# Dot products of fetched expert rows placed behind the gates' first pass

## The chip, the cores and the metric

The kernel runs on one core of a Trainium2 chip. The metric is the device time of one execution in microseconds; lower is better. Five engines run their own instruction queues and wait for each other through semaphores: TensorE (PE in the profile, its weight loads PEld), VectorE (DVE), ScalarE (ACT), GpSimd (POOL) and SyncE (SP), which only issues transfers here. Each engine works through its queue in the order in which the compiler's scheduler has put it.

## What is computed

One layer of a decoder step over 512 prompt tokens and 32 sample tokens: a mixer (retention and a convolution module, one input and one output projection), a layer norm, then a retrieval of experts, a second norm. The change lies in the retrieval:

```python
q = (xb @ w_query).reshape(PEER_BLOCK, PEER_HEADS, PEER_DQ)
...
s1 = jnp.einsum('phd,hkd->phk', q1, sub_keys_1)
s2 = jnp.einsum('phd,hkd->phk', q2, sub_keys_2)
v1, i1 = lax.top_k(s1, PEER_TOPK)
v2, i2 = lax.top_k(s2, PEER_TOPK)
...
idx = e1 * N_KEYS + e2
gate = jax.nn.softmax(sv.astype(jnp.float32), axis=-1).astype(xb.dtype)
u = jnp.take(peer_u, idx, axis=0)
act = jax.nn.gelu(jnp.einsum('phkd,pd->phk', u, xb), approximate=False)
vv = jnp.take(peer_v, idx, axis=0)
return jnp.einsum('phk,phkd->pd', gate * act, vv)
```

There are 8 heads with 16 picks each, so every token takes 128 of 16,384 experts. Each expert has a row of 1,024 numbers in `peer_u` and one in `peer_v`.

## The kernel before

The tokens are treated in two ways.

**Fetched rows.** The first chunk of 128 prompt tokens, the 32 samples (group "s") and the second chunk of 128 prompt tokens (group "b") fetch the rows of the experts they picked. `gather` does this, one slot at a time. A slot is: an indirect transfer by POOL's queue (L564) of one row pair of 8 KB for each of 128 partitions into a tile `g`, of which the pool has three buffers; on DVE the dot product of the `u` half with the token (L567); on ACT the Gelu and its product with the gate (L569, L570); on DVE the weighted add of the `v` half into `acc` (L575). The first chunk has 128 slots, started in the mixer and done before the part that follows here. The samples are folded onto 128 partitions and have 32 slots, the second chunk has 128. `fetched()` runs these two groups one after the other, each closed by sums over the folded parts (samples only, L933 and L934), a residual add (L582), the norm of L445 to L453 and a store by SP (L585).

**Dense scores.** The last two chunks, 256 tokens, are computed against all experts instead, 128 blocks of 128 experts. `scores_of` loads a block of `u` (L771) and multiplies (L774); Gelu follows on ACT; `place(e)` is the block's slice of one of four tiles, Gb, Gc, Ga and Gd (32, 20, 44 and 32 blocks). Then the scores are multiplied by the gates, which are zero but for the picked experts, and `v_stage` multiplies the result with a block of `v` rows loaded by SP (L889) and adds it up in four PSUM tiles `pB` (L893). The loads of both kinds share five buffers.

**The gates.** `build` makes the gate matrix for eight tokens at a time. DVE compares indices and writes one-hot tiles A (L847), M (L849) and B (L852), two buffers each; PE multiplies them, three matmuls a token (L858), into one of two PSUM tiles; DVE drains each PSUM tile. `first_keys` is the first pass, over the 96 blocks of Gb, Gc and Ga, with 96 columns a matmul: three instructions drain four tokens (L870 once, L872 twice). `last_keys` is the second pass, over the 32 blocks of Gd, drained by ACT (L878). The blocks of Gc and Gd have their scores computed after their gates: `s_stage` puts Gelu into W (ACT, L884) and multiplies it in on DVE (L885).

**Order.** The source calls the first pass, then `run` interleaves `phases()` (one block of `v_stage`, at times with an `s_stage` or a step of the second pass) with two steps of `fetched()`. This is not yet the order on the engines: a scheduler places each instruction by its dependencies and by modelled times, so that slots of the samples come ahead of the first pass and in the middle of it on DVE. `behind(ins, other)` is a helper that forbids the scheduler to put `ins` ahead of `other`; it adds no data. At the end two layer norms read `pB` and store the last two chunks.

Of the kernel before, what the change touches and what calls it, by code (L numbers as in the profile page):

```python
# [14 lines left out]
OP = mybir.AluOpType  # L15
# [3 lines left out]
D = 1024  # L19
# [72 lines left out]
def tile_step(ctx: ExitStack, tc: tile.TileContext, a, o):  # L92
    nc = tc.nc
    V, S, T, G = nc.vector, nc.scalar, nc.tensor, nc.gpsimd
# [68 lines left out]
    def behind(ins, other):  # L163
        tc.add_manual_dep(ins.ins, other.ins.name, mybir.DependencyInfo(
            mybir.DependencyClass.NoSync, mybir.DependencyReason.DATA), reason="order")
# [297 lines left out]
    def mix_mm(n, gT, y, c0, wo, xT=None):  # L463

        banks_ = [mmps(), mmps()]
        if xT is not None:
            for q in range(2):
                residual(banks_[q], xT, range(q * 4, q * 4 + 4), c0)
        for src, k0 in ((y, 4), (gT, 0)):
            for q in range(2):  # L470
                for s in range(2):
                    for k in range(4):
                        last = T.matmul(banks_[q][:n, s * 256:(s + 1) * 256], src[:, k, c0:c0 + n],
                                        wo[q * 2 + s][:, k0 + k, :], start=(xT is None and k0 == 4 and s == 0 and k == 0),
                                        stop=(k0 == 0 and s == 1 and k == 3), skip_group_check=True)
        return banks_, last
# [31 lines left out]
    def retrieve(q_of, hs, w, r, E, gate, e0, later=None):  # L508
# [47 lines left out]
        V.reciprocal(sm[:n], sm[:n])  # L556
        V.tensor_mul(gate[:n, e0:e0 + nh], ex[:n], sm[:n].unsqueeze(2).to_broadcast([n, nh, TK]))

    def gather(x1, idx, gate, acc, slots):

        for k in slots:
            t = (gx.tile([128, 2 * D], F32, name="g") if x1 is x1_0 and k < KX and k % 4 == 3 else
                 gp.tile([128, 2 * D], F32, name="g"))
            G.indirect_dma_start(out=t, out_offset=None, in_=a["uv"],  # L564
                                 in_offset=bass.IndirectOffsetOnAxis(ap=idx[:, k:k + 1], axis=0))
            act = gw.tile([128, 2], F32, name="act")
            V.scalar_tensor_tensor(t[:, :D], t[:, :D], 1.0, x1, op0=OP.mult, op1=OP.mult, accum_out=act[:, 0:1])  # L567
            wgt = gw.tile([128, 1], F32, name="wgt")
            S.activation(act[:, 1:2], act[:, 0:1], AF.Gelu)  # L569
            S.activation(wgt, act[:, 1:2], AF.Copy, scale=gate[:, k:k + 1])  # L570
            v = t[:, D:]
            if k == slots[0]:
                S.activation(acc, v, AF.Copy, scale=wgt)
            else:
                V.scalar_tensor_tensor(acc, v, wgt, acc, op0=OP.mult, op1=OP.add)  # L575
            yield
# [10 lines left out]
    def run(*gens):  # L587

        live = list(gens)
        while live:  # L590
            for g in list(live):
                for _ in range(g[1]):
                    if next(g[0], "end") == "end":
                        live.remove(g)
                        break
# [53 lines left out]
    pm, last = mix_mm(128, g0, y0, 0, wo)  # L649
# [90 lines left out]
    mix_b(NS + 2 * C, C)  # L740
    caches()
    gather0 = gather(x1_0, I0, g0_gates, acc0, range(PH * TK))
    for _ in range(KX):
        next(gather0)
# [96 lines left out]
    def build(bt, e0, ne, nt):  # L841


        pt = None
        for t1 in range(0, ND, TB):
            A = bt.tile([128, NK, TB], BF, name="A")
            V.tensor_tensor(A, iot, e1T[:, t1:t1 + TB].unsqueeze(1).to_broadcast([128, NK, TB]), op=OP.is_equal)  # L847
            M = bt.tile([128, ne, TB], BF, name="M")
            V.tensor_tensor(M, iot[:, e0:e0 + ne],  # L849
                            e2T[:, t1:t1 + TB].unsqueeze(1).to_broadcast([128, ne, TB]), op=OP.is_equal)  # L850
            B = bt.tile([128, 3, ne, TB], BF, name="B")
            V.tensor_tensor(B, M.unsqueeze(1).to_broadcast([128, 3, ne, TB]),  # L852
                            gtT[:, :, t1:t1 + TB].unsqueeze(2).to_broadcast([128, 3, ne, TB]), op=OP.mult)
            for t in range(t1, t1 + TB):
                if t % nt == 0:
                    pt = pdn.tile([128, nt, ne], F32, name="mm")
                for q in range(3):
                    T.matmul(pt[:, t % nt], A[:, :, t - t1], B[:, q, :, t - t1], start=(q == 0), stop=(q == 2))  # L858
                if t % nt == nt - 1:
                    yield pt, slice(t - nt + 1, t + 1)  # L860

    def first_keys():

        with tc.tile_pool(name="bt", bufs=2, reuse_waits="tile") as bt:
            for pt, ts in build(bt, 0, E0S[3], 4):
                for g in range(3):
                    to = GW[g][:, :, ts]
                    part = pt[:, :, E0S[g]:E0S[g + 1]].rearrange("p t e -> p e t")
                    if g == 1:
                        V.tensor_copy(to, part)  # L870
                    else:
                        V.tensor_mul(to, to, part)  # L872

    def last_keys():

# [20 lines left out]
    def phases():  # L896
        for e in range(EG[0]):
            v_stage(e)
            if e < EG[1]:
                s_stage(E0S[1] + e)  # L900
            yield
        gbs.close()
        gd = ctx.enter_context(tc.tile_pool(name="gd", bufs=1, side="right", reuse_waits="tile"))
        GW[3] = gd.tile([128, EG[3], ND], F32, name="Gd")
        b = last_keys()
        more = iter(range(E0S[3], NK))
        for e in range(E0S[1], E0S[3]):
            v_stage(e)
            if next(b, "end") == "end":
                for _ in range(1):  # L910
                    k = next(more, None)
                    if k is not None:
                        s_stage(k)
            yield
        for e in range(E0S[3], NK):
            v_stage(e)
            yield

    def fetched():
        t = dn.tile([128, D], F32, name="yt")  # L920
        finish(x1_0, [acc0[:, 0:512], acc0[:, 512:]], 128, [(0, 128, o[0][0, 0:128])], t)
        yield
        for g, c0, dst in (("s", 0, o[1].rearrange("b i d -> (b i) d")), ("b", NS, o[0][0, 128:256])):
            w_, r_ = GSP[g]
            x1g = dn.tile([128, D], F32, name="x1g")
            for b in range(r_):
                nc.scalar.dma_start(x1g[b * w_:(b + 1) * w_], x1_dram[c0:c0 + w_])
            ac = per.tile([128, D], F32, name="acc")
            yield from gather(x1g, Ig[g], GTg[g].rearrange("p h k -> p (h k)"), ac, range(128 // r_))
            t = dn.tile([128, D], F32, name="yt")  # L930
            for b in range(1, r_):
                part = dn.tile([128, D], F32, name="yt")
                S.activation(part[:w_], ac[b * w_:(b + 1) * w_], AF.Copy)  # L933
                V.tensor_add(ac[:w_], ac[:w_], part[:w_])  # L934
            finish(x1g, [ac[:, 0:512], ac[:, 512:]], w_, [(0, w_, dst)], t)
            yield

    first_keys()
    run((phases(), 1), (fetched(), 2))
    for b in range(2):  # L940
        t = uvp.tile([128, D], F32, name="uv")
# [50 lines left out]
```

## Time and profile before

| | us |
|---|---|
| three runs | 1721.68, 1728.95, 2358.62 |
| median of them | 1728.95 |
| the profiled execution | 1726.13 |
| its span, first to last instruction | 1724.4 |

The profile is one execution. Each row of a window query is a stretch of the span with the time each engine was busy in it, the clock granted to TensorE, and what the transfers took. A timeline row has the start in us, the duration in us, engine, line, operation, the output and inputs by the program's names with buffer numbers left out, how many instructions are merged, and in brackets the idle time before it and what ended it. A DVE instruction's row may overlap the next one's start by a tenth of a us, so rates are taken from start to start. fp32 matmuls show as two records each, so L774 has 16 records a block.

The stages of the span, by their main lines:

| from to, us | stage |
|---|---|
| 0 to about 480 | mixer, and the first chunk's retrieval and first slots |
| to 870 | queries and picks, dense scores, the first chunk's remaining slots; the samples' first gather is issued at 804 |
| 873 to 1062 | the first pass |
| 1062 to 1187 | `v_stage` with the `s_stage` of Gc |
| 1187 to 1376 | `v_stage`, then with the second pass |
| 1376 to 1548 | `v_stage` with the `s_stage` of Gd |
| 1548 to 1710 | `v_stage` alone on PE |
| 1710 to 1724 | closing norms and stores |

### The profile page before, as it was taken

What the parts mean: (1) busy time and instruction counts of PE and PEld (TensorE: products, weight loads), DVE (VectorE), ACT (ScalarE), POOL (GpSimd) and SP (SyncE); (2) the same over time, 40 slices, a digit from 0 to 9 for tenths busy, and PEclk for the clock granted to TensorE, in tenths of its full rate; (3) what the DMA queues carried; (4) which work ended last, traced back from release to release, by engine and by line L of the source; (5) the groups of instructions that cost most, each with busy time, mean ns of one, the idle gap of its engine ahead of it and who ended that gap; (6) DMA issues with size and microseconds to landing.
All of it is one profiled execution on the core that took longest, in us unless ns stands there. A gap on an engine that the chain in (4) does not pass through costs nothing.

```text
span 1724.4 us, 20025 instructions
## 1 busy us (share of the span) xinstructions
PE 1610.5 (93%) x7014; PEld 1123.9 (65%) x7014; DVE 1282.7 (74%) x3044; ACT 391.4 (23%) x1091; POOL 386.5 (22%) x335
## 2 busy tenths in 40 slices
PE   7899999969599999999998888999999999999997
PEld 6887566547455678888886565665557776664443
DVE  4949998898759999999679899665466665556631
ACT  1324541452223233333210011111111111111100
POOL 1001321445312222201211113222122222232200
PEclk9899999989889999999985656999999999999999
DMA  9459778978987799955965436999877899999952
GB/s 364 156 204 377 256 266 291 346 273 291 355 310 284 260 368 351 350 191 211 367 228 183 171 98 226 405 354 362 335 294 283 292 368 364 367 358 398 421 209 98
DMA packets 99537, 503.71 MB, mean 292 GB/s; under 512 B 10183, under 2 KB 21191, under 8 KB 56549
## 3 DMA queue, kind: packets, MB, share of 16 engines
q0 software_dynamic: 42240, 305.12, 47.3%
q1 hardware_dynamic: 50749, 189.96, 29.8%
q10 hardware_dynamic: 6448, 7.36, 1.3%
q8 instruction: 55, 0.90, 0.2%
q14 instruction: 45, 0.37, 0.1%
HBM read 497.03 MB, written 5.80 MB: 292 GB/s over the span
## 4 chain that ended last, share of the span: by engine, by line
PE 55%; DVE 30%; DMA 8%; issue 3%; POOL 1%; ACT 1%; SPq 0%; DVEq 0%; ACTq 0%; POOLq 0%
PE pB L893 26%; PE sp L774 13%; PE mm L196 8%; DVE acc L575 6%; DVE g L567 5%; PE mm L858 5%; DMA g<-in_uv_dram,I 4%; DVE B L852 2%; DMA g<-in_w_in_dram 1%; DVE pick L549 1%; DVE oh L546 1%; DMA out_dram<-keys 1%; DMA keys<-in_state_retention_dram 1%; DVE score L503 1%; PE mm L306 1%
## 5 line engine op out<-in xcount | busy, mean ns | idle before, releaser
L774 PE MATMUL sp<-x1T,uv 128*128 128x256 f32 x2048 | 467.5, 384 | 11.3 <-ACT Ga L820 5.8
L774 PEld LDWEIGHTS sp<-x1T,uv 128*128 128x128 f32 x2048 | 390.0, 193 | 83.6 <-issue 15.7
L575 DVE SCALAR_TENSOR_TENSOR acc<-g,wgt,acc 128x1024 f32<-128x1024 f32 x285 | 364.8, 1280 | 79.5 <-ACT wgt L570 78.7
L564 POOL DMA_INDIRECT g<-in_uv_dram,Ib x128 | 155.9, 1218 | 502.4 <-DVE acc L575 404.9
L564 POOL DMA_INDIRECT g<-in_uv_dram,I x128 | 160.4, 1254 | 436.7 <-DVE acc L575 207.3
L567 DVE SCALAR_TENSOR_TENSOR g<-g,x1g 128x1024 f32<-128x1024 f32 x160 | 195.3, 1222 | 63.9 <-DMA g<-in_uv_dram,Ib 51.5
L858 PE MATMUL mm<-B,A 128*128 128x96 bf16 (+1 forms) x1536 | 195.6, 300 | 25.3 <-DVE Ga L872 25.3
L569 ACT ACTIVATE act<-act 128x1 f32<-128x1 f32 x288 | 58.0, 201 | 679.5 <-DVE g L567 679.4
L858 PEld LDWEIGHTS <-A 128*128 128x128 bf16 x1536 | 162.6, 151 | 69.9 <-DVE Ga L872 33.6
L196 PE MATMUL mm<-x1T,w 128*128 128x384 f32 (+1 forms) x512 | 181.1, 508 | 0.7 <-ACT on L426 0.7
L567 DVE SCALAR_TENSOR_TENSOR g<-g,x 128x1024 f32<-128x1024 f32 x128 | 155.6, 1216 | 26.4 <-DMA g<-in_uv_dram,I 24.3
L893 PE MATMUL pB<-uv,Ga 128*128 128x512 f32 x352 | 156.1, 593 | 0.0
L196 PEld LDWEIGHTS mm<-x1T,w 128*128 128x128 f32 x512 | 98.0, 194 | 73.8 <-issue 42.1
L893 PE MATMUL pB<-uv,Gb 128*128 128x512 f32 x256 | 118.0, 613 | 0.4 <-DVE Gb L872 0.4
L893 PEld LDWEIGHTS pB<-uv,Ga 128*128 128x128 f32 x352 | 66.8, 190 | 71.3 <-issue 69.8
L893 PE MATMUL pB<-uv,Gd 128*128 128x512 f32 x256 | 110.0, 592 | 0.0
L893 PEld LDWEIGHTS pB<-uv,Gd 128*128 128x128 f32 x256 | 48.6, 190 | 61.2 <-issue 60.7
L893 PEld LDWEIGHTS pB<-uv,Gb 128*128 128x128 f32 x256 | 50.2, 198 | 56.3 <-issue 54.6
L847 DVE TENSOR_TENSOR A<-iot,e1T 128x1024 bf16<-128x1024 bf16 x64 | 43.9, 687 | 49.3 <-PE mm L858 49.3
L564 POOL DMA_INDIRECT g<-in_uv_dram,Is x32 | 35.9, 1123 | 183.3 <-DVE acc L575 131.4
L893 PE MATMUL pB<-uv,Gc 128*128 128x512 f32 x160 | 72.7, 607 | 0.0
L196 PE MATMUL mm<-g,w 128*128 128x160 f32 (+1 forms) x512 | 69.7, 294 | 3.0 <-ACT score L522 2.6
(274 smaller groups left out, 1695.0 us busy)
## 6 DMA issues: line engine op xcount, KB each, us to landing
uv<-in_ut_dram SPq DMA_DIRECT2D x128, 512.0 KB
uv<-in_uv_dram SPq DMA_DIRECT2D x128, 512.0 KB
w<-in_w_in_dram SPq DMA_DIRECT2D x18, 1024.0 KB
w<-in_w_query_dram SPq DMA_DIRECT2D x16, 1024.0 KB
w<-in_w_out_dram SPq DMA_DIRECT2D x7, 1024.0 KB
g<-in_uv_dram,I POOLq DMA_INDIRECT x128, 7.7
keys<-in_state_retention_dram ACTq DMA_DIRECT2D x4, 512.0 KB
out_dram<-keys SPq DMA_DIRECT2D x4, 512.0 KB
```

Source lines behind the costliest of these rows:

```text
L196: T.matmul(p[:, :n], w[m // 2][:, k, (m % 2) * 128:(m % 2 + 1) * 128], xT[:, k, c0:c0 + n], start=(k == 0), stop=(k == 7))
L306: mm = T.matmul(p[:n, q * 256:(q + 1) * 256], xT[:, k, c0:c0 + n], w[q][:, k, :], start=(k == 0), stop=(k == 7))
L503: V.match_replace(s, dst[:, 0:8], s, -3.0e38)
L564: G.indirect_dma_start(out=t, out_offset=None, in_=a["uv"], in_offset=bass.IndirectOffsetOnAxis(ap=idx[:, k:k + 1], axis=0))
L567: V.scalar_tensor_tensor(t[:, :D], t[:, :D], 1.0, x1, op0=OP.mult, op1=OP.mult, accum_out=act[:, 0:1])
L569: S.activation(act[:, 1:2], act[:, 0:1], AF.Gelu)
L575: V.scalar_tensor_tensor(acc, v, wgt, acc, op0=OP.mult, op1=OP.add)
L774: T.matmul(sp, u[:, k], x1T[:, k, NG2:], start=(k == 0), stop=(k == 7))
L847: V.tensor_tensor(A, iot, e1T[:, t1:t1 + TB].unsqueeze(1).to_broadcast([128, NK, TB]), op=OP.is_equal)
L852: V.tensor_tensor(B, M.unsqueeze(1).to_broadcast([128, 3, ne, TB]), gtT[:, :, t1:t1 + TB].unsqueeze(2).to_broadcast([128, 3, ne, TB]), op= ...
L858: T.matmul(pt[:, t % nt], A[:, :, t - t1], B[:, q, :, t - t1], start=(q == 0), stop=(q == 2))
L893: T.matmul(pB[b][q], W[:, b * 128:(b + 1) * 128], vt[:, q * 512:(q + 1) * 512], start=False, stop=(e == NK - 1), skip_group_check=True)
```

## The change

`first_keys` returns its last multiply (the last L872), which is kept in a list. Every dot product that `gather` records after that is ordered behind it on DVE. The first chunk's slots are recorded earlier, while the list is empty, so they are untouched; the 160 dots of the samples and the second chunk are all recorded later. Gathers are not ordered, nor are the steps after the dot, other than by what they need.

```diff
+    fence = []
+
     def gather(x1, idx, gate, acc, slots):
...
-            V.scalar_tensor_tensor(t[:, :D], t[:, :D], 1.0, x1, op0=OP.mult, op1=OP.mult, accum_out=act[:, 0:1])
+            dot = V.scalar_tensor_tensor(t[:, :D], t[:, :D], 1.0, x1, op0=OP.mult, op1=OP.mult, accum_out=act[:, 0:1])
+            if fence:
+                behind(dot, fence[0])
...
-                        V.tensor_mul(to, to, part)
+                        last = V.tensor_mul(to, to, part)
+        return last
...
-    first_keys()
+    fence.append(first_keys())
     run((phases(), 1), (fetched(), 2))
```

## The prediction

> **What bounds the kernel now.** I read the page first, then stretches of the span by window, then single rounds of DVE and PE in the timeline.
>
> ```profile
> span 1724.4 us, 20025 instructions
> PE 1610.5 (93%) x7014; PEld 1123.9 (65%) x7014; DVE 1282.7 (74%) x3044; ACT 391.4 (23%) x1091; POOL 386.5 (22%) x335
> ...
> q0 software_dynamic: 42240, 305.12, 47.3%
> ...
> PE 55%; DVE 30%; DMA 8%; issue 3%; POOL 1%; ACT 1%; SPq 0%; DVEq 0%; ACTq 0%; POOLq 0%
> ```
>
> The chain of waits is mostly PE, but 30% of it is DVE, so there are stages that DVE sets. The windows say which. I cut them at five events: first matmul of the gates' first pass, its end, the last W multiply (L885) of group c, the first and the last of group d, and the end of the value-row loads.
>
> ```profile
> 873.40:1061.60 188.20, 162.52 (x814) 123.44 (x812) 172.44 (x358) 20.10 (x63) 34.56 (x28) 0.61 0.47 160
> 1061.60:1187.40 125.80, 125.80 (x494) 82.93 (x495) 79.86 (x120) 17.75 (x67) 32.35 (x26) 0.98 0.95 362
> 1187.40:1376.20 188.80, 188.80 (x1057) 115.51 (x1056) 117.56 (x180) 27.71 (x90) 43.04 (x34) 0.99 0.84 310
> 1376.20:1548.20 172.00, 172.00 (x609) 115.49 (x608) 98.38 (x136) 26.25 (x97) 46.13 (x35) 1.00 0.94 362
> 1548.20:1697.00 148.80, 148.80 (x349) 65.81 (x348) 69.89 (x85) 14.05 (x53) 23.08 (x25) 1.00 0.84 327
> ```
>
> Columns: stretch and length, busy us of PE, PE's weight loads, DVE, ACT, POOL, then PE's granted clock, the DMA share, GB/s. In the first stretch, the gates' first pass, DVE is busy 172 of 188 us and PE has gaps. From 1061.6 to the end of the matmuls PE has none. The DMA engines are half idle in the first stretch and nearly full in most of what follows.
>
> **What the change takes out of the first pass.** One round of that pass (8 tokens, two drains) on DVE:
>
> ```profile
> 942.09 0.28 DVE L872 TENSOR_TENSOR Gb<-Gb,mm 128x128 f32<-128x128 f32 x1
> ...
> 945.62 1.22 DVE L567 SCALAR_TENSOR_TENSOR g<-g,x1g 128x1024 f32<-128x1024 f32 x1
> ...
> 946.76 1.28 DVE L575 SCALAR_TENSOR_TENSOR acc<-g,wgt,acc 128x1024 f32<-128x1024 f32 x1
> 947.96 0.28 DVE L872 TENSOR_TENSOR Gb<-Gb,mm 128x128 f32<-128x128 f32 x1
> ```
>
> A round takes 947.96 - 942.09 = 5.87 us. The slot in it (dot product and accumulate of one fetched row per token) is 947.96 - 945.62 = 2.34; the pass itself needs 3.53. The built program of the changed kernel has no slot before the last L872; the kernel before has 40 there, some of them ahead of the pass. So DVE needs 3.53 per round, and PE becomes the next limit:
>
> ```profile
> 873.41 8.71 PE L858 MATMUL mm<-B,A 128*128 128x96 bf16 x48
> 881.94 5.95 PE L774 MATMUL sp<-x1T,uv 128*128 128x256 f32 x16
> 887.73 4.44 PE L858 MATMUL mm<-B,A 128*128 128x96 bf16 x24
> ...
> 895.46 6.58 PE L858 MATMUL mm<-B,A 128*128 128x96 bf16 x36
> 901.86 6.22 PE L774 MATMUL sp<-x1T,uv 128*128 128x256 f32 x16
> 907.92 4.44 PE L858 MATMUL mm<-B,A 128*128 128x96 bf16 x24
> ...
> 1061.59 11.79 PE L893 MATMUL pB<-uv,Gb 128*128 128x512 f32 x20 [0.38 <-DVE Gb L872]
> ...
> 895.00:900.00 5.00, 5.00 (x29) 4.07 (x29) 3.30 (x8) 0.88 (x3) 1.67 (x1) 1.00 0.56 172
> ```
>
> Start to start, 48 matmuls take 881.94 - 873.41 = 8.53 us, 36 take 6.40: 0.178 each, 4.27 a round. That is above DVE's 3.53, so PE sets the round. The pass has 768 of these matmuls, 24 of them before 873: 744 x 0.178 = 132 us. Beside them PE runs here three score groups (5.79, about 3.5 and 6.06 start to start: 15) and ten value matmuls, which cost between 4 and 12 us by the row at 1061.59 (20 records, half of them per matmul); I take 6. The pass would end at 873.4 + 132 + 15 + 6 = 1026.6 instead of 1061.6: **35 us earlier**. Bounds: DVE alone, 31 rounds x 3.53 = 109 us for the 132, gives 58; a PE that loses a drain of 0.6 (three instructions in the round above, 942.09 on) in each of 31 rounds gives 17.
>
> The clock is not what makes these matmuls slow. The last row above covers 5 us at granted clock 1.00, and the 36 matmuls that begin in them take the same 0.178. [...]
>
> **What it moves.** From the end of the pass to the last W multiply PE has no gap, so that stretch keeps its 1548.2 - 1061.6 = 486.6 us and moves forward whole: last W at 1513. The order of the two built programs decides the rest. Between the end of the pass and the last W, DVE has 95 slots in both, at nearly the same places among the W multiplies. So nothing of the displaced work is taken up there: before, 25 of 160 slots come behind the last W; after, **65** do. What is queued behind a waiting dot on DVE is what it was; PE waits for DVE only through W and the drains, as before. On POOL three gathers stand landed behind the wait and the rest wait for their buffers. ACT's two steps a slot move with it, on an engine at 23%. The samples' closing steps, which lay in the pass, come between the last W of group c and the first of group d, in place of about five slots; DVE is busy 118 of 189 us there (third window), so I cost that at nothing; without that cover it would be the 10 to 40 us of the last rival. SP's store of the samples' output moves behind 18 of 29 value-row loads; the store of the second chunk moves behind all.
>
> The tail before:
>
> ```profile
> 1548.23 0.42 DVE L885 TENSOR_TENSOR Gd<-Gd,W 128x256 f32<-128x256 f32 x1 [1.43 <-ACT W L884]
> ...
> 1549.85 1.23 DVE L567 SCALAR_TENSOR_TENSOR g<-g,x1g 128x1024 f32<-128x1024 f32 x1
> ...
> 1647.12 1.23 DVE L567 SCALAR_TENSOR_TENSOR g<-g,x1g 128x1024 f32<-128x1024 f32 x1 [0.59 <-DMA g<-in_uv_dram,Ib]
> ...
> 1648.96 1.28 DVE L575 SCALAR_TENSOR_TENSOR acc<-g,wgt,acc 128x1024 f32<-128x1024 f32 x1 [0.60 <-ACT wgt L570]
> ...
> 1656.74 1.23 DVE L453 TENSOR_TENSOR yt<-yt,lnb 128x1024 f32<-128x1024 f32 x1
> 1710.04 0.70 DVE L445 BATCH_NORM_STATS2 lst<-pB 128x6 f32<-128x512 f32 x1 [52.07 <-PE pB L893]
> ...
> 1717.95 1.28 DVE L453 TENSOR_TENSOR uv<-uv,lnb 128x512 f32<-128x512 f32 x2
> ```
>
> The stream of slots now ends 52 us before PE does; that is the whole cover for what is moved. 25 dots from 1549.85 to 1647.12 are (1647.12 - 1549.85) / 24 = 4.05 us a slot, and 40 slots at that price are 162 us. A slot waits for its gather:
>
> ```profile
> 1000.00:1060.00 60.00, 48.08 (x260) 36.80 (x260) 59.53 (x129) 8.08 (x20) 12.78 (x9) 0.50 0.34 109
> 1560.00:1640.00 80.00, 80.00 (x188) 35.46 (x187) 50.90 (x61) 9.94 (x40) 18.73 (x20) 1.00 1.01 416
> ...
> DMA to landing us min/median/max: 5.5/6.1/7.4
> DMA to landing us min/median/max: 8.2/8.3/9.6
> ```
>
> The two landing lines are the gathers of the same two windows: 6.1 us at DMA share 0.34, 8.3 at 1.01. Three buffers go round: dot start to end of accumulate 3.0 (1647.12 to about 1650.2), some 0.3 until POOL issues, and the landing, divided by three: 3.9 at 8.3, 3.1 at 6.1. DVE's own chain allows no less than 3.0. While PE still loads value rows (148.8 us from the last W) I take 4.05; after that 3.3, nearer to 3.1 because half the demand is gone, and not 3.1 because 305.12 MB over 288 gathers is 1.06 MB, at 3.3 us 320 GB/s of the 416 seen.
>
> The sum: last W 1513.2; first dot 1.6 later, 1514.8; 36 slots x 4.05 = 146, up to the end of the loads at 1662; the other 28 x 3.3 = 92; end of the last accumulate 3.0 later: 1756. DVE's program then has the second chunk's output norm and, behind its first operation, the norm of the last two chunks, for which PE has been ready since about 1710 - 35 = 1675. Alone the first takes 1657.97 - 1650.2 = 7.7 and the second up to 1719.2 - 1710.0 = 9.2, of which some 7.5 is DVE's work; the store behind it is 1724.4 - 1719.2 = 5.2. That is 20. End 1776. The execution took 1726.13 us for a span of 1724.4, so 1.7 more: **1778 us**, 3.0% over that execution; the median of the runs, 1728.95, lies 2.8 above it, and I let that be. With 28 slots between 3.0 and 4.05 the term is 84 to 113, and with the pass between 17 and 58 the forecast's own range is 1747 to 1817 at the far ends, 1758 to 1800 where I believe it.
>
> **The rivals.**
>
> *The stream stays hidden (faster).* PE remains last: 1726.1 - 35 = 1691 us. It decides where 65 slots and their norm fit into PE's remaining 162 us (1710.0 - 1548.2), 2.4 us a slot. DVE's own 3.0 speaks against it. Chance 0.04.
>
> *DVE's floor holds for the whole tail (no change).* If gathers win against value-row loads, 64 x 3.03 = 194: 1514.8 + 194 + 3 + 20 + 1.7 = 1734. Against it: in the 80 us at 416 GB/s a slot took 4.05. Chance 0.10.
>
> *The matmuls of the pass become fast (no change).* [...] Chance 0.08.
>
> *SP's store holds up PE (slower still).* SP runs in order, and loads behind a store wait with it:
>
> ```profile
> SPq L585 <- DVE yt L453: 136.3, 1, 136.3
> ```
>
> Before, SP stood at the samples' store for 136 us, harmless in the pass, where PE needs few rows. After, the store stands among loads that PE consumes at 3.4 us each, with five buffers, 17 us, of cover. It decides if the samples' last slots and their norm come more than that late; POOL and ACT steps lie in that chain. Each us beyond goes to PE and the last W alike; I take 10 to 40: 1788 to 1818. Chance 0.14.
>
> **How the numbers follow.** Forecast 0.64, rivals 0.04, 0.10, 0.08, 0.14. A measurement of this kernel tells about 2% from no change: 1694 and 1763. Of the forecast 0.60 lies above 1763 and 0.04 below, so slower 0.60 + 0.14 = 0.74, same 0.04 + 0.10 + 0.08 = 0.22, faster 0.04. The range 1746 to 1812 leaves out the faster rival, the lower half of the second and the upper end of the last.
>
> **What would show it.** In the new profile: rounds of about 4.3 us in the pass with PE busy and no L567 in it; the last L872 near 1027; last W near 1513; 65 dots behind it, first about 4 us, later about 3.3 apart; the wait for pB at 52.07 gone, DVE and gathers in place of PE at the end of the chain of waits. The prediction is wrong if the pass keeps 188 us, if the tail's dots come under 2.6 us apart, or if PE shows gaps on value rows between the pass and the last W.

## The result and the profile after

| | us |
|---|---|
| six runs of the changed kernel | 1785.2 to 1792.74 |
| median of them | 1787.58 |
| its profiled execution, span | 1786.38, 1784.6 |
| median of the kernel before, beside them | 1728.76 |
| ratio after to before | 1.0353, 95% interval 1.0327 to 1.038 |

The change makes the kernel 3.5% slower. One of the six runs of the kernel before took 2358.62 us; it counts in the median, but the ratio is that of the means of the other runs. The page of the changed kernel, its first lines and the shares of the chain of waits:

```profile
span 1784.6 us, 20041 instructions
PE 1605.5 (90%) x7014; PEld 1125.1 (63%) x7014; DVE 1287.8 (72%) x3044; ACT 391.8 (22%) x1091; POOL 386.4 (22%) x335
...
q0 software_dynamic: 42240, 305.12, 45.0%
...
PE 52%; DVE 23%; DMA 15%; issue 6%; POOL 2%; ACT 2%; SPq 0%; DVEq 0%; POOLq 0%; ACTq 0%
```

Every engine has nearly the same busy time as before in a span that is 60.2 us longer (1784.6 - 1724.4). In the chain DVE gave up 7 points, and DMA and "issue" (time in which the profile shows no wait) gained 10 together. The windows, cut at the events of the prediction's rows (the pass's last L876, the last W multiply of group c at L890, the first and the last of group d, the end of the value-row loads), and two more for what now follows. The first row starts a little earlier than its counterpart: with DVE's first drain, at 863.39, where the prediction's row starts with PE's matmuls of the pass, at 873.41.

```profile
863.00:1022.30 159.30, 158.95 (x828) 126.87 (x826) 107.84 (x276) 1.89 (x5) 0.00 (x0) 0.63 0.05 17
1022.30:1147.40 125.10, 125.07 (x494) 82.69 (x495) 78.04 (x119) 19.55 (x69) 32.43 (x26) 0.98 0.92 352
1147.40:1343.20 195.80, 195.80 (x1057) 118.74 (x1056) 123.52 (x188) 31.91 (x92) 41.74 (x35) 0.96 0.82 300
1343.20:1515.20 172.00, 172.00 (x609) 115.53 (x608) 98.36 (x136) 26.27 (x99) 44.52 (x35) 1.00 0.95 362
1515.20:1664.00 148.80, 148.80 (x349) 65.84 (x348) 93.81 (x113) 18.79 (x76) 35.23 (x37) 1.00 1.01 412
1664.00:1763.20 99.20, 15.57 (x37) 6.61 (x35) 68.14 (x83) 13.44 (x54) 36.46 (x26) 0.59 0.79 294
1763.20:1784.60 21.40, 0.00 (x0) 0.00 (x0) 15.37 (x27) 4.40 (x7) 2.14 (x6) 0.50 0.19 74
```

Columns as before: PE, PE's weight loads, DVE, ACT, POOL, granted clock, DMA share, GB/s. Three readings. First, the pass: PE is busy 158.95 of 159.3 us, POOL does nothing and the transfers move 17 GB/s, where before they moved 160. The slots are gone from the pass. Second, the four stretches in which PE is busy throughout have nearly their old lengths. Third, behind the loads there is a new stretch of 99 us in which PE has 15.57 us of work left. The timelines of PE and DVE give the events:

```profile
868.39 4.41 PE L862 MATMUL mm<-B,A 128*128 128x96 bf16 x24
...
1022.35 0.33 DVE L876 TENSOR_TENSOR Ga<-Ga,mm 128x176 f32<-128x176 f32 x1
...
1515.23 0.42 DVE L890 TENSOR_TENSOR Gd<-Gd,W 128x256 f32<-128x256 f32 x1 [1.19 <-ACT W L889]
...
1516.85 1.22 DVE L569 SCALAR_TENSOR_TENSOR g<-g,x1g 128x1024 f32<-128x1024 f32 x1
...
1763.17 1.23 DVE L569 SCALAR_TENSOR_TENSOR g<-g,x1g 128x1024 f32<-128x1024 f32 x1
1765.00 1.29 DVE L579 SCALAR_TENSOR_TENSOR acc<-g,wgt,acc 128x1024 f32<-128x1024 f32 x1 [0.60 <-ACT wgt L574]
...
1768.13 2.47 DVE L445 BATCH_NORM_STATS2 lst<-pB 128x6 f32<-128x512 f32 x4
```

PE's run of 744 matmuls of the pass starts at 868.39 (873.41 before). The pass ends at 1022.35 (1061.60 before), the last W is at 1515.23 (1548.23), so the gain is 39 us at the first place and 33 at the second. Behind the last W stand 65 dots; the first starts at 1516.85, the last at 1763.17. The norm statistics of `pB`, at 1768.13, have no idle time for PE ahead of them any more; before it was 52.07 us.

### The profile page after: what moved, and what is told of

It is laid out like the page before. It is cut to its first block, busy times and chain, and to the rows that moved or that the text cites. A ratio compares the mean times of both kernels' runs of the same rounds, so it can differ in the third digit from the quotient of the medians.

```text
span 1784.6 us, 20041 instructions
## 1 busy us (share of the span) xinstructions
PE 1605.5 (90%) x7014; PEld 1125.1 (63%) x7014; DVE 1287.8 (72%) x3044; ACT 391.8 (22%) x1091; POOL 386.4 (22%) x335
## 4 chain that ended last, share of the span: by engine, by line
PE 52%; DVE 23%; DMA 15%; issue 6%; POOL 2%; ACT 2%; SPq 0%; DVEq 0%; POOLq 0%; ACTq 0%
PE pB L898 16%; PE sp L778 14%; PE mm L862 10%; DMA g<-in_uv_dram,Ib 9%; PE mm L196 8%; DVE acc L579 6%; DVE g L569 4%; DMA g<-in_uv_dram,I 4%; DVE pick L549 1%; DVE oh L546 1%; POOL g L566 1%; DMA w<-in_w_in_dram 1%; DMA out_dram<-keys 1%; DVE blk L266 1%; PE mm L306 1%
## 5 line engine op out<-in xcount | busy, mean ns | idle before, releaser
L778 PE MATMUL sp<-x1T,uv 128*128 128x256 f32 x2048 | 466.1, 384 | 11.4 <-ACT Gb L829 5.8
L862 PE MATMUL mm<-B,A 128*128 128x96 bf16 (+1 forms) x1536 | 192.0, 301 | 0.0
L898 PE MATMUL pB<-uv,Gc 128*128 128x512 f32 x160 | 77.1, 637 | 0.0
L876 DVE TENSOR_TENSOR Gb<-Gb,mm 128x128 f32<-128x128 f32 x64 | 18.1, 283 | 80.0 <-PE mm L862 51.0
```

The lines of the kernel that those rows point to most:

```text
L778: T.matmul(sp, u[:, k], x1T[:, k, NG2:], start=(k == 0), stop=(k == 7))
L876: last = V.tensor_mul(to, to, part)
L898: T.matmul(pB[b][q], W[:, b * 128:(b + 1) * 128], vt[:, q * 512:(q + 1) * 512], start=False, stop=(e == NK - 1), skip_group_check=True)
```

## The experiments

In the expectations, theory A is the prediction's own: the wait takes slots out of the pass, the pass shortens, and the slots that were moved come back behind the last W at the pace of their gathers. A1 is the form of it in which that pace is a matter of shared bandwidth alone. B stands for the rival that the loss comes from something else than these slots. All edits are made on the changed kernel; all ratios are to the kernel before on the same chip, where its median was 1721.45 us beside the first four runs named here (88 slots, from 28, from 13, half rows) and 1719.6 beside the others. Times of different runs are therefore best compared by their ratios.

**The moved slots left out.** The second chunk gets 88 of its 128 slots; 25 dots stay behind the last W, as many as in the kernel before.

```diff
-            yield from gather(x1g, Ig[g], GTg[g].rearrange("p h k -> p (h k)"), ac, range(128 // r_))
+            yield from gather(x1g, Ig[g], GTg[g].rearrange("p h k -> p (h k)"), ac, range(32 if r_ > 1 else 88))
```

> The changed kernel with the second chunk's last 40 slots left out (its output is then not complete). Theory A, the moved slots make a longer tail behind the last W multiply: 25 slots are left there, the stream ends at about 1515 + 100 + 3 = 1618, long before PE (1664 + 14), and PE sets the end again: span about 1692, time about 1690 to 1696, below the kernel before by the 39 us that the first pass gained less the 6 us the stretch behind it lost. Theory B, the loss lies in how DVE's waits hold up PE between the pass and the last W: the slots left out lie behind that stretch, so the time stays above 1750.

1691.66 us, ratio 0.9812 (0.9767 to 0.9857). Without the 40 slots the loss of 3.5% turns into a gain of 1.9%; on the kernel before, 1728.95, that is 1696 us, near the 1691 that the first rival gave for a hidden stream. The time lies in the range that theory A gave. So the gain of the pass is real, and the loss lies in the slots behind the last W. B falls.

**How many slots wait.** The samples have 32 slots. Three kernels let the first of them run ahead as the scheduler likes and order the rest behind the pass; `Ig["b"]` is the second chunk's index tile.

```diff
-            if fence:
+            if fence and (idx is Ig["b"] or k >= 28):
```

The other two have 13 and 20 in place of 28. In the kernel before, 13 slots lie ahead of the pass's first drain and 27 more in the pass.

> Only the samples' slots from the 28th on and the second chunk's wait for the pass; 28 slots stay ahead of its end, 12 fewer than before. Theory A: the pass loses 12 slots of 2.34 us, 28 us; the tail has 38 slots, ending near 1521 + 150 + 3 + 8 = 1682, just before PE's end near 1682: time about 1698, 1.8% under the kernel before. Theory B, any wait of the dots harms: above 1729.

> The 13 slots that the kernel before has ahead of the first pass's first drain stay where they were; only those in the pass wait. Theory A: the pass still ends near 1022 to 1026; the tail has 53 slots, ends near 1515 + 1.6 + 146 + 16 x 3.5 + 3 = 1722, and the time is about 1740 to 1745, some 45 us under the changed kernel. If it is the waiting in the pass rather than the count in the tail, it stays near 1787.

> Slots from the samples' 20th on wait; 20 stay ahead of the pass's end. Theory A: the pass ends near 1026, the last W near 1515; the tail has 45 slots, ends near 1516.6 + 36 x 4.03 + 8 x 3.62 + 3 = 1694, the norms follow: about 1714, between the 1707 with 28 slots ahead and the 1740 with 13, and PE's end no longer sets it.

| slots ahead of the pass's end | pass ends | last W | dots behind it | last dot | ratio to before (95%) |
|---|---|---|---|---|---|
| 40 (before) | 1061.60 | 1548.23 | 25 | 1647.12 | 1 |
| 28 | 1034.56 | 1526.38 | 38 | 1677.92 | 0.9929 (0.9902 to 0.9957) |
| 20 | 1026.76 | 1519.49 | 45 | 1695.40 | 0.998 (0.9963 to 0.9997) |
| 13 | 1023.80 | 1509.33 | 53 | 1714.64 | 1.0104 (1.006 to 1.0147) |
| 0 (the change) | 1022.35 | 1515.23 | 65 | 1763.17 | 1.0353 (1.0327 to 1.038) |

The medians of the three are 1707.25, 1716.1 and 1740.29 us. The last two came out as theory A had them; with 28 the gain is 0.7% where 1.8% was expected, and the last W comes 5 us later than the 1521 of the expectation. Of the five counts 28 has the lowest time. The first 12 slots that are moved bring 27 us of pass (1061.60 to 1034.56), and behind the last W they cost nothing: the last dot is at 1677.92, and PE is still at work. The end of the chain of waits of that kernel:

```profile
1525.93 164.81 PE pB L898 x384
```

PE's value matmuls run for 164.81 us from 1525.93, to 1690.7, 13 us behind the last dot. Each of those slots brings 2.25 us, about the 2.34 of DVE that it takes. The next 8 bring 1 us each (1034.56 to 1026.76) and the last 20 together 4.4 (to 1022.35): DVE is by then no longer what the pass waits for. Each of the 27 dots that they put behind the last W (38 to 65) costs a whole slot there once the stream outlasts PE.

**What sets the pace behind the last W: half of the value rows.** From block 84 on only half of each block's `v` row is loaded, and both matmuls of a block use that half.

```diff
+        half = 512 if e >= 84 else 0
...
-        nc.sync.dma_start(vt, a["uv"][e * NK:(e + 1) * NK, D:])
+        nc.sync.dma_start(vt[:, :D - half], a["uv"][e * NK:(e + 1) * NK, D:2 * D - half])
...
-                T.matmul(pB[b][q], W[:, b * 128:(b + 1) * 128], vt[:, q * 512:(q + 1) * 512],
+                T.matmul(pB[b][q], W[:, b * 128:(b + 1) * 128], vt[:, 0:512] if half else vt[:, q * 512:(q + 1) * 512],
```

> The changed kernel, with only half of each value row loaded for the last 44 blocks and that half used twice (so the last two chunks' output is another). PE's work is the same, the transfers in the tail are fewer. Theory A1, the tail's slots are paced by the bandwidth that gathers share with value rows: 416 GB/s less 76 for the halved loads leaves 340, a slot of 1.06 MB comes to about 3.2 us instead of 3.95 over 37 slots, so 25 to 30 us less than the changed kernel: about 1757 to 1763. Theory A2, three gather buffers and a fixed landing time pace them: no change, 1784 to 1790.

1778.83 us, ratio 1.0324 (1.0279 to 1.0369): well above A1's time. It is also a little below the times given for A2, but by its ratio it is not told from the changed kernel (1.0353), as A2 has it. The window from the last W to the end of the loads, of this kernel:

```profile
1512.20:1661.00 148.80, 148.80 (x349) 65.81 (x348) 95.69 (x115) 18.85 (x77) 49.13 (x38) 1.00 0.93 341
```

The transfers move 341 GB/s against 412 in the same stretch of the changed kernel, yet their share only falls from 1.01 to 0.93, and a slot takes 3.95 us in place of 4.02. Each row of a load shrank from 4 KB to 2 KB with the count of rows unchanged. Between 1530 and 1660 the loads' share of the transfer engines fell from 37.9% to 24.1%, less than by half, and the gathers took 69.6% in place of 63.1% for nearly the same number of rows. So this run shows that bytes are not the measure; it does not show what a slot would take beside truly idle transfer engines.

**One buffer more.** A fourth buffer for the slots of the samples and the second chunk.

```diff
+    g4 = []
...
-            t = (gx.tile([128, 2 * D], F32, name="g") if x1 is x1_0 and k < KX and k % 4 == 3 else
-                 gp.tile([128, 2 * D], F32, name="g"))
+            pool = gx if x1 is x1_0 and k < KX and k % 4 == 3 else gp
+            if x1 is not x1_0 and k % 4 == 3:
+                pool = g4[0]
+            t = pool.tile([128, 2 * D], F32, name="g")
...
+    g4.append(ctx.enter_context(tc.tile_pool(name="g4", bufs=1)))
```

> The changed kernel with a fourth gather buffer, made of memory that the first pass leaves. With half the value rows the tail's slots kept 3.97 us against 4.03, so sharing the bandwidth is not what sets that pace alone. Theory A2, three buffers going round a landing of some 8 us set it: four of them allow (3.0 + 0.3 + 8.5) / 4 = 2.95, below DVE's own 3.03, so the tail's 57 slots (the order puts 8 more ahead of the last W) need about 175 to 190 us: stream end near 1515 + 185, time about 1720 to 1735. Theory A1, the transfer engines are full (share 1.01) and a fourth gather only waits longer: 57 slots at 4.0 then 3.6, end near 1515 + 149 + 20 x 3.6 + 3, time about 1757 to 1762, less than the changed kernel only by the 8 slots moved.

1733.74 us, ratio 1.0085 (1.0054 to 1.0117): three quarters of the loss come back. The windows from 1515 on, four us ahead of this kernel's last W (1518.96):

```profile
1515.00:1660.00 145.00, 144.40 (x337) 62.13 (x335) 98.27 (x118) 20.14 (x81) 39.57 (x40) 1.00 1.01 420
1660.00:1715.00 55.00, 29.78 (x65) 11.50 (x64) 39.39 (x48) 7.59 (x32) 20.04 (x15) 0.80 0.93 370
```

and from the transfers between 1530 and 1660 the gathers, with their count and the median us from issue to landing:

```profile
g<-in_uv_dram,Ib POOLq DMA_INDIRECT x36, 11.4
```

A slot takes 3.66 us beside the loads (4.02 with three buffers) and 3.36 behind them (3.62), and 57 dots are left behind the last W, 8 fewer. The last dot comes 43 us sooner (1719.77 against 1763.17). About 31 us of that are the eight slots, which the order on DVE puts ahead of the last W in this kernel; the faster pace gives 15 (56 intervals of 3.58 us on the mean in place of 3.85), and the later last W takes some back. The time lies in A2's range, but partly by luck, for A2's pace of 2.95 did not come: the stream was to end near 1700. The round of buffers sets the pace, as the prediction had it: (3.0 + 0.3 + 11.4) / 4 = 3.68 against 3.66 beside the loads. But a fourth buffer at the old landing of 8.5 us would have reached DVE's 3.0. Instead the landing rose to 11.4 at 420 GB/s: the transfer engines were full before (share 1.01), and the gathers win their time from the value rows. Between 1530 and 1660 the gathers' share of the transfer engines rose from 63.1% to 67.1%, and that of the loads fell from 37.9% to 34.4%. PE shows it: its value matmuls behind the last score group take 171.7 us (1518.34 to 1690.07), where the kernel with 88 slots needs 164.81 for the same work.

**The best of both.** The fourth buffer, for the slots that wait only, and the wait from slot 20 on.

> As the run before with a fourth gather buffer for the waiting slots; the order leaves 37 in the tail. The stream then ends before PE even at 4.03 a slot (1516.6 + 148 = 1665 against 1677), so PE sets the end: about 1691 + 2 = 1693, 2% under the kernel before. If a fourth gather in flight holds up PE's value rows, PE shows gaps and it stays above 1705.

1700.73 us, ratio 0.99 (0.9862 to 0.9937): 1% under the kernel before, between the two times of the expectation. Against the kernel with 28 slots ahead (0.9929) the intervals overlap. DVE's timeline near its end:

```profile
1650.38 1.29 DVE L589 SCALAR_TENSOR_TENSOR yt<-x1g,acc 128x512 f32<-128x512 f32 x2
...
1683.04 0.70 DVE L445 BATCH_NORM_STATS2 lst<-pB 128x6 f32<-128x512 f32 x1 [29.93 <-PE pB L901]
```

The second chunk's last slot is done at 1650.38, and DVE then stands 29.93 us for PE: the stream of slots is hidden again, and PE ends last. Its profiled span stays 7 us above that of the kernel with 88 slots (1699.5 against 1692.5), although its last W comes 3 us sooner (1515.06 against 1518.25). Its chain of waits behind the last W has one reason, value rows that came late:

```profile
1514.60 61.83 PE pB L901 x144
...
1624.62 15.67 DMA uv<-in_uv_dram
1644.14 41.45 PE pB L901 x96
```

From 1514.60 to 1685.59 PE needs 171 us for what the chain of the 28-slot kernel, and likewise that of the 88-slot one, has as one run of 164.81. So the fourth gather in flight does hold up PE's value rows, by 6 us. The other reason is the order on DVE, where the chunk's closing multiply and add with the norm's weights, 1.22 us each from 1686.29 on, stand among those of the last two chunks: from PE's end to the end of the span it takes 13.9 us, against 9.9.

**What makes the pass's matmuls slow.** B is laid out so that the 96 columns of one matmul lie side by side; before, one column lies 16 bytes behind the other (eight tokens of two bytes).

```diff
-            B = bt.tile([128, 3, ne, TB], BF, name="B")
+            B = bt.tile([128, 3, TB, ne], BF, name="B").rearrange("p q t e -> p q e t")
```

> The changed kernel with B laid out so that the 96 columns of a matmul of the pass lie side by side instead of 16 bytes apart; the matmul's work is the same. If the stride of the columns costs the 0.178 us, the matmuls of the pass come under 0.10 and DVE's round of 3.53 (or more, as B's write is now the strided one) sets the pass: it ends up to 23 us earlier and so does the kernel, 1764 to 1787. If the clock or the weight loads cost it, 0.178 stays and so does the time, 1784 to 1790.

2060.8 us, ratio 1.1988 (1.1951 to 1.2025), far outside both times of the expectation. The timeline of one round of the pass in this kernel:

```profile
1001.48 11.63 DVE L856 TENSOR_TENSOR B<-M,gtT 128x2304 bf16<-128x2304 bf16 x1
...
1013.67 2.14 PE L862 MATMUL mm<-B,A 128*128 128x96 bf16 x24 [11.58 <-DVE Ga L876]
```

the window around it:

```profile
1000.00:1060.00 60.00, 10.64 (x120) 9.67 (x120) 60.00 (x42) 0.00 (x0) 0.00 (x0) 0.50 0.00 0
```

and the write of B in the timeline of the changed kernel:

```profile
941.27 1.35 DVE L856 TENSOR_TENSOR B<-M,gtT 128x2304 bf16<-128x2304 bf16 x1
```

24 matmuls take 2.14 us, with the end of the last one in it. From start to start, over the whole pass, they come 0.081 us apart at a granted clock of 0.50 (643 pairs) and 0.060 apart at 1.00 (86 pairs). With the columns 16 bytes apart, in the pass of the changed kernel, they come 0.178 apart at 0.50 (613 pairs) and as much at 1.00 (124 pairs). The weights lie as before in both. So the layout sets that price, and neither the clock nor the weight loads do: at the same clock of 0.50 it is 0.178 against 0.081. Why columns 16 bytes apart cost more no run shows. The write pays instead: the same 2304 elements take DVE 11.63 us in place of 1.35, and DVE, busy 60.00 of 60 us, sets the pass.

## Why the prediction was right, step by step

The forecast of 1778 us lies 9.6 below the median, inside its own range, and the mechanism held: nothing of the moved work is taken up on the way, 65 dots come behind the last W, and they end the kernel. By its terms, against the span of 1784.6:

- *The pass becomes PE's.* Predicted end 1026.6, measured 1022.35, so 39 us earlier instead of 35. PE is busy all but 0.35 us of it. The length came out to within 1 us: 153.2 us were predicted from the first of the 744 matmuls on, and 868.39 to 1022.35 are 154.0 with the last drain. The matmuls took 132.3 for the 132; that the rest fits is partly luck, for the scores took 11.2 in place of 15, as some of them ran earlier, and the value matmuls 9.7 in place of 6. The 4 us come from the start, which the prediction left at 873.4: it moved 5 us forward.
- *From the pass to the last W, 486.6 us kept.* Measured 492.9 (1515.23 - 1022.35), 6.3 more, all of it between the last W of group c and the first of group d, where 195.8 stand for 188.8 and the granted clock was 0.96 for 0.99. The samples' norm lies there now, but PE shows no gap in it. In the other kernels, but for the one with dense columns, the whole stretch came out between 485.5 and 493.6 without following the number of slots; the cause stays open. The prediction's rival put 10 to 40 us on a late store here; these 6.3 are not from the store, as shown below.
- *36 slots at 4.05 beside the loads.* Measured 37 intervals at 4.02: right.
- *28 slots at 3.3 behind them.* Measured 27 intervals at 3.62. This is the term that was mis-sized: all 64 intervals took 246.3 us where the sum has 238.2, 8.1 of the 8.6 us by which it fell short; the later last W (+2.0) and the norms (-1.7) nearly cancel. Three intervals are one round of a buffer, and the traces give its four parts for each slot. The means in us:

| | dot's start to accumulate's end | to the next issue | issue's start to landing | landing to dot | round |
|---|---|---|---|---|---|
| beside the loads, 1530 to 1660, 33 slots | 3.12 | 0.27 | 8.62 | 0.02 | 12.03 |
| behind them, 1672 to 1757, 24 slots | 3.37 | 0.37 | 6.82 | 0.20 | 10.76 |

  The prediction took 3.0 for the first part and 0.3 for the second, so its 3.3 a slot leaves 6.6 for the landing, 9.9 in all. What it lacked is spread over all parts, 0.4 of it in the first. There 0.1 was misread from its own lines, where 1647.12 to the end of the accumulate at 1648.96 + 1.28 is 3.1; the rest is the order on DVE, which behind the loads has two dots ahead of two accumulates at three places, so that a buffer comes free late:

```profile
1669.91 1.22 DVE L569 SCALAR_TENSOR_TENSOR g<-g,x1g 128x1024 f32<-128x1024 f32 x1 [3.13 <-DMA g<-in_uv_dram,Ib]
...
1671.07 2.68 DVE L579 SCALAR_TENSOR_TENSOR acc<-g,wgt,acc 128x1024 f32<-128x1024 f32 x2
```

  POOL's own time to issue a gather changed too. The first row of this view, behind the loads, has it (least, median, most, in ns):

```profile
L566 POOL DMA_INDIRECT g<-in_uv_dram,Ib x25: 932/1672/1978, 1672.6 to 1756.9; - x25
...
DMA to landing us min/median/max: 5.7/6.5/8.0
```

  The same view of 1530 to 1660, beside the loads:

```profile
L566 POOL DMA_INDIRECT g<-in_uv_dram,Ib x33: 932/932/934, 1530.5 to 1656.8; - x33
...
DMA to landing us min/median/max: 8.2/8.5/9.0
```

  This issue is a part of the landing and must not be added to it, for the landing is counted from the issue's start: the gather issued at 1704.66, in 1.94 us, is in the chain of waits from 1704.66 on for 6.86 us, and its dot starts at 1711.55. When it is slow can be read in the timelines:

```profile
1699.25 1.22 DVE L569 SCALAR_TENSOR_TENSOR g<-g,x1g 128x1024 f32<-128x1024 f32 x1
1699.60 1.67 POOL L566 DMA_INDIRECT g<-in_uv_dram,Ib  x1 [2.72 <-DVE acc L579]
```

  The issue begins while a dot runs on DVE. From 1020 on the changed kernel has 157 issues: of 53 that took over 1.2 us, 51 begin inside a dot or an accumulate, and of the 104 shorter ones 2 do. Beside the loads DVE mostly stands waiting when POOL issues; behind them the next slot has often landed. The kernel with half the value rows tells the two apart. There, beside the loads, 13 of 32 issues were slow, all of them inside a step of DVE. So slow issues go with DVE's steps and not with the end of the loads. They do not explain the landing: from 1664 on, the 14 gathers with a slow issue landed after 6.5 us on the mean, the 12 others after 7.2. What they do to the pace no run varied, and it stays open.
- *20 us of closing norms.* From the end of the last accumulate, 1766.3, to the end of the span: 18.3.

**The rivals.** The hidden stream did not come; with all slots it needed 2.4 us a slot, and no stretch behind the last W named here went under 3.36. DVE's floor for the whole tail fell with the measured paces; even a fourth buffer did not reach it. That the matmuls of the pass become fast was the author's estimate, and the changed kernel does not show it: PE was busy 158.95 us of 159.3 in the pass, at 0.178 a matmul throughout and whatever the clock. SP's store fell by its own timeline:

```profile
1188.17 3.76 SPq L894 DMA_DIRECT2D uv<-in_uv_dram  x2
1191.98 0.42 SPq L589 DMA_DIRECT2D out_dram<-yt  x1
1195.04 4.37 SPq L894 DMA_DIRECT2D uv<-in_uv_dram  x2
```

SP issues value rows at 1188, the samples' store at 1191.98 and value rows again at 1195, and DVE's norm for it was done at 1186. The store came in its turn and waited for nothing; the list of SP's waits has one long wait at this line, and it is for the second chunk's store at the end, with only the closing stores behind it:

```profile
SPq L589 <- DVE yt L453: 114.3, 1, 114.3
```

## What to carry to other kernels

Before you take work out of a crowded stage, find the stage that will do it instead and the price there: an engine's gap counts only if it lies ahead of the end that the work would set. Slots in the pass cost 2.34 us of DVE each, and next to nothing (4.4 us of pass for the last 20) once PE is the limit there; behind the last W they cost 3.6 to 4.0, because three buffers going round set the pace there, beside the loads over a full set of transfer engines (share 1.01). So move only as much as still fits under the engine that ends last: of the kernels run here, 12 slots of 40, or 20 with one buffer more.

## What the runs showed of the hardware that was not expected

- In the pass of the changed kernel a matmul of 96 bf16 columns took 0.178 us with columns 16 bytes apart, at a granted clock of 0.50 as at 1.00; with dense columns it took 0.081 at 0.50 and 0.060 at 1.00. The dense layout, in which the elements of a column for two neighbouring tokens lie 192 bytes apart and not 2, raised one multiply of 2304 bf16 elements from 1.35 to 11.63 us.
- PE busy nearly without a gap (158.95 of 159.3 us) did not go with a high granted clock: 0.63 over the changed kernel's pass, against 0.96 to 1.00 in the four stretches behind it, with PE as busy there.
- Value rows in 2 KB pieces and the gathers beside them took 0.93 of the transfer engines at 341 GB/s; with 4 KB pieces it was 1.01 at 412.
- In the changed kernel, from 1020 us on, a gather's issue on POOL that began inside a dot or an accumulate of DVE took 1.67 to 1.98 us (51 of 53); one that began outside took 0.93 to 1.14 (102 of 104).
